# The two meta rows times w_out: fp32 on four column tiles in place of split fp32r

## The chip, the cores and the metric

The kernel runs on one core of one Trainium2 chip. A core has a matrix engine (TensorE, PE in the profile, with its weight loads listed apart as PEld), three engines for elementwise work (VectorE or DVE, ScalarE or ACT, GpSimd or POOL), and queues that issue DMA transfers; here nearly all transfers go through SyncE's queue (SP). The metric is the device time of one execution in microseconds, lower is better; the time of a kernel is the median of its runs.

## The reference

The kernel computes one layer of a hybrid decoder trunk for 1024 tokens of width 1024, with 16 meta tokens put in front. After a first LayerNorm the layer does this:

```python
z = h @ w_in + b_in                      # q, k, v, conv input, gates
y_attn = attention(q, k, v) @ w_attn_proj
y_conv = conv_branch(c_in) @ w_conv_proj
mixed = sigmoid(g_attn) * y_attn + sigmoid(g_conv) * y_conv
h = layer_norm(ALPHA * h + mixed @ w_out, ln1_g, ln1_b)
up = causal_dwconv(h @ ffn_w_up, ffn_dw, ffn_dw_b)      # 3 taps
u, g = split(up)
out = layer_norm(ALPHA * h + (gelu(g) * u) @ ffn_w_down, ln2_g, ln2_b)
```

Only the 1024 token rows are returned. Of the 16 meta rows just the last two are needed behind `mixed`: the causal convolution of the feed-forward part has three taps, so the first token row reaches back to them. These two rows, a 2 x 1024 matrix, have to be multiplied with `w_out` (1024 x 1024) like the 1024 others, and this product is what the change concerns.

## The kernel before

**Numbers in two parts.** Nearly every product is made to fp32 accuracy from fp32r operands. A value `x` is split into `hi`, its fp32r rounding, and `lo = x - hi`; ACT makes `hi` and DVE makes `lo` (`split`, L300 to L303). A product is then three matmuls per block of the contraction: `lo*hi`, `hi*hi`, `hi*lo` (`product`, L340 to L344).

**Order of the work.** The code gives each instruction a rank (`tc.cur_priority`, `rank`), and a planner lays out each engine's instructions by simulated time: whatever is ready and has the lowest rank goes next. Where a fixed order is wanted, `after` ties one instruction behind another. An engine, and a DMA queue, runs its instructions strictly in the order that came out; an instruction that waits holds up those behind it on its engine.

**Stages.** First the projection `z`, then attention and convolution, then the two branch projections with the gates (L1172 on PE, `merge` on DVE and ACT, up to about 506 us), then the row stage (498 to 605 us), then the up product (to 1035 us), then the down product.

**The branch projections** loop over eight blocks `m` of 128 channels and over four groups `g` of token columns. `merge` writes the mixed values, split, to `RHC` and `RHO`. For the first group it also puts the two meta rows aside in the tile `pair`: for each channel block four columns, two of the fp32r part (L1187, ACT) and two of the rest (L1188, DVE).

**The weights** `w_out` are loaded in eight blocks of 128 rows and split by `prep_wo`. Blocks 0 to 3 are loaded into parts of the tile `FA` (`early`, at columns 2064, 3088, 0 and 1024), block 4 into `FA` from column 4112, block 5 into `OB` from column 3072, blocks 6 and 7 into the two buffers `wr` that all weights pass through. The split parts go to `OA`, `RX`, `RW` and `w`. A raw block is free again when it has been split; the next user of the two `wr` buffers is the first block of up weights.

**The row stage** calls `out_rows(i)` for the row blocks in the order 3, -1, 7, 2, 6, 0, 4, 1, 5, where -1 stands for the two meta rows. A row block of 128 is multiplied with `w_out` in two halves of 512 columns, 24 matmuls a half, on a PSUM bank out of a ring of three (`ps_w`, tag `mm`, shared with the projections). DVE adds the residual rows, which were loaded from `h0d` (L1345), and takes the statistics; the block is normalized (L271 to L274 and L1369), written to `h1d`, and turned by PE transposes (L1379) between the halves of a later block. Block 3 is turned between the halves of block 7, block 7 between those of block 2, and the meta rows behind the second half of block 2.

**The meta rows** have their own path in `out_rows` (n = 2, L1355 to L1364). A half is 16 matmuls: per channel block one with all four columns of `pair` as the stationary operand and `hi` of `w_out` as the moving one (L1356), and one with the two fp32r columns and `lo` (L1357). So the bank has four rows: rows 0 and 1 hold `hi*hi + hi*lo`, rows 2 and 3 hold `lo*hi`. ACT copies the four rows to `OB` from column 3072 (L1358). Rows 2 and 3 must be added to rows 0 and 1; since DVE works within a partition, a DMA first moves them to partitions 0 and 1 of `FA` (the load at L1363, added at L1364), as it does for the residual rows of `h0d` (added at L1362).

Of the kernel before, what the change touches and what calls it, by code (L numbers as in the profile page):

```python
# [23 lines left out]
F = mybir.dt.float32  # L24
R = mybir.dt.float32r
AF = mybir.ActivationFunctionType
OP = mybir.AluOpType
AX = mybir.AxisListType

P = 128  # L30
D = 1024
KC = D // P
# [81 lines left out]
def tile_hybrid_layer(  # L114
# [3 lines left out]
    nc = tc.nc  # L118
# [5 lines left out]
    def load(o, i):  # L124
        return nc.sync.dma_start(out=o, in_=i)
# [5 lines left out]
    def f32(ap):  # L131
        return ap.bitcast(F)
# [6 lines left out]
    @contextmanager  # L139
    def rank(p):  # L140

        saved = tc.cur_priority
        tc.cur_priority = p
        yield
        tc.cur_priority = saved


    const = ctx.enter_context(tc.tile_pool(name="const", bufs=1, side="left"))
# [8 lines left out]
    FA = arena.tile([P, 6144], F, name="FA")  # L157
    RHC = arena.tile([P, KC * T], R, name="RHC")
    RHO = arena.tile([P, KC * T], R, name="RHO")
    OB = arena.tile([P, 4 * U], F, name="OB")  # L160
# [8 lines left out]
    h0d = dpool.tile([U, D], F, name="h0d")  # L169
# [11 lines left out]
    start = ExitStack()  # L181
# [114 lines left out]
    def wraw(shape):  # L296
        return wraw_p.tile(shape, F, name="wr", tag="wr")
# [13 lines left out]
    def wsp_flat(dtype=R):  # L311
        t = wsp(dtype)
        return [t[:, o:o + D] for o in W_FLAT]
# [279 lines left out]
    for a, b in ((0, 400), (400, J_LEN)):  # L593
        ps = pat.tile([P, 512], F, name="ps_v", tag="o" if a == 0 else "mm", bufs=1 if a == 0 else 3)
# [204 lines left out]
    ps = pat.tile([P, 512], F, name="ps_vm", tag="t", bufs=2)  # L799
    after(nc.tensor.transpose(ps[:64, :P], vmT, ident), q1[-1])  # L800
    src = ps[:64, :P].rearrange("p (g d) -> p g d", d=HD)
    nc.scalar.copy(vm[:64, :, 0], src)
    nc.vector.tensor_tensor(vm[:64, :, 1], src, f32(vm[:64, :, 0]), OP.subtract)
    for q4 in range(2):
        ps = pat.tile([P, 512], F, name="ps_v4", tag="t", bufs=2)
# [3 lines left out]
        src = ps[:, :].rearrange("p (n g d) -> p n g d", g=2, d=HD)  # L809
        for g in range(NKV):  # L810
            hi, lo = (V[:, q4 * 4:q4 * 4 + 4, g, i] for i in range(2))
# [21 lines left out]
    ps = pat.tile([P, 512], F, name="ps_s2", tag="t", bufs=2)  # L833
    for h in range(NH):
        g, r = divmod(h, 4)
        o = ps[:2, h * 16:(h + 1) * 16]
# [50 lines left out]
    ps = pat.tile([P, 512], F, name="ps_o", tag="o", bufs=1)  # L887
# [16 lines left out]
    for i in range(NB):  # L904
# [5 lines left out]
        for g in range(NKV):  # L910
# [6 lines left out]
            for r in range(4):  # L917
                ps = pat.tile([P, 512], F, name="ps_s", tag="s", bufs=2)
# [11 lines left out]
            hs = slice(g * 4, g * 4 + 4)  # L930
# [9 lines left out]
            for c, kb in bands:  # L940
                ps = pat.tile([P, 512], F, name="ps_t", tag="t", bufs=2)
# [20 lines left out]
    order = [1, "c2"] + list(range(2, 5)) + ["c3"] + list(range(5, 16))  # L962
# [166 lines left out]
        return t[:, 0:8192].rearrange("p (t j x) -> p t j x", t=2, j=2)[:, :, j, cols]  # L1129

    w_out_v = w_out.rearrange("(k p) c -> k p c", p=P)
    wo = {}

    def prep_wo(k, raw=None, behind=None):
        if k < 4:
            hi, lo = (OA[:, OA_WO + k * 2048 + x:OA_WO + k * 2048 + x + 1024] for x in (0, 1024))
        elif k < 6:
            hi, lo = ((RX[:, RX_WO:], RW)[k - 4][:, x:x + 1024] for x in (0, 1024))
        else:
            hi, lo = wsp_flat()  # L1140
        if raw is None:
            raw = wraw([P, D])
            load(raw, w_out_v[k])
        split(raw, hi, lo, behind)
        wo[k] = (hi, lo)

    pair = const.tile([P, KC, 4], R, name="pair")
    g_next = [0]

    GS = [(FA, i * 516) for i in range(4)]  # L1150
# [11 lines left out]
    for m in range(KC):  # L1162
        hi, lo = weights([P, KC, P], lambda raw: load(raw, w_ab[m]))

        def branch(i, g, tag, bufs):
            a, b = PG[g]
            ps = pat.tile([P, 512], F, name="ps_p", tag=tag, bufs=bufs)
            rhs = (oo, conv)[i]
            for k in range(4):
                ah, al = hi[:, 4 * i + k], lo[:, 4 * i + k]  # L1170
                for j, (x, hl) in enumerate(((ah, 0), (ah, 1), (al, 0))):
                    nc.tensor.matmul(ps[:, :b - a], x, rhs(k, hl, a, b), start=k + j == 0, stop=k == 3 and j == 2)  # L1172
            return ps[:, :b - a]

        def merge(g, psa, psb):
            a, b = PG[g]
            n = b - a
            with rank(RK_EVAC):
                t = gslot()[:, :, :n]
                ins = load(t, dram(sgd, m * P * U + a, [[U, P], [KC * P * U, 2], [1, n]]))  # L1180

                ta, tb = t[:, 0], t[:, 1]
                nc.vector.scalar_tensor_tensor(ta, ta, 1.0, psa, OP.add, OP.mult)
                nc.vector.scalar_tensor_tensor(tb, tb, 1.0, psb, OP.add, OP.mult)
                nc.vector.tensor_tensor(ta, ta, tb, OP.add)
                if g == 0:
                    nc.scalar.mul(pair[:, m, 0:2], ta[:, 0:2], 0.5)  # L1187
                    nc.vector.scalar_tensor_tensor(pair[:, m, 2:4], ta[:, 0:2], 0.5, f32(pair[:, m, 0:2]),  # L1188
                                                   OP.mult, OP.subtract)
                v = ta[:, n - 256:].rearrange("p (t x) -> p t x", t=2)  # L1190
                h = mixed2(g, m, 0)
                last_act = nc.scalar.mul(h, v, 0.5)
                nc.vector.scalar_tensor_tensor(mixed2(g, m, 1), v, 0.5, f32(h), OP.mult, OP.subtract)
            return ins, last_act

        if m < KC - 1:
            pa = [branch(0, g, "mm", 3) for g in range(2)]
            for g in range(4):
                if g > 1:
                    pa.append(branch(0, g, "mm", 3))  # L1200
                last_gate, last_act = merge(g, pa[g], branch(1, g, "t", 2))
        else:
            pa = [branch(0, g, "mm", 3) if g < 3 else branch(0, g, "s", 2) for g in range(4)]
            for g in range(4):
                last_gate, last_act = merge(g, pa[g], branch(1, g, "t", 2))
        if m in (2, 3):
            raw = (FA[:, 4112:5136], OB[:, 3072:4096])[m - 2]
            load(raw, w_out_v[m + 2])
            prep_wo(m + 2, raw, last_act)
        if m < 4:  # L1210
            early.append(FA[:, E_AT[m]:E_AT[m] + 1024])
            after(load(early[m], w_out_v[m]), last_gate)
# [109 lines left out]
    def out_rows(i, between=(), work=()):  # L1322


        n, u = (P, 2 + i * P) if i >= 0 else (2, 0)
        if n == P:
            o = r_next[0] % 2 * 1024
            r_next[0] += 1
            whole = RT[:, o:o + 1024]
            load(whole, h0d[u:u + n, :])  # L1330
        else:
            whole = OB[:, 3072:4096]
        r = whole[:n]
        order = WO_ORDER if i != 5 else (0, 1, 2, 3, 6, 7, 4, 5)
        turned = None
        st = small.tile([P, 2, 6], F, name="st")
        pin = line if i in (0, 4, 1, 5) else lambda ins: ins
        for half in range(2):
            hs = slice(half * 512, half * 512 + 512)
            ps = pat.tile([P, 512], F, name="ps_w", tag="mm", bufs=3)  # L1340
            if n == P:
                last = product(ps, [(mixed(i, k, 0), mixed(i, k, 1), wo[k][0][:, hs], wo[k][1][:, hs])
                                    for k in order], turned)
                with rank(RK_TURN):
                    pin(nc.vector.tensor_tensor(r[:, hs], ps, r[:, hs], OP.add))  # L1345
                    pin(nc.vector.bn_stats(st[:, half], r[:, hs]))
                turned = None
                if len(between) > half:
                    turned = turn(*between[half], behind=[last])
                if half == 0:  # L1350
                    for f, *x in work:
                        f(*x)
                continue

            for j, k in enumerate(order):  # L1355
                nc.tensor.matmul(ps[:4], pair[:, k], wo[k][0][:, hs], start=j == 0, stop=False)  # L1356
                last = nc.tensor.matmul(ps[:2], pair[:, k, 0:2], wo[k][1][:, hs], start=False, stop=j == KC - 1)  # L1357
            nc.scalar.copy(whole[:4, hs], ps[:4])  # L1358
        if n < P:
            q = FA[:4, 0:1024]  # L1360
            load(q[0:2], h0d[0:2, :])
            nc.vector.tensor_tensor(r, r, q[0:2], OP.add)  # L1362
            load(q[0:2], whole[2:4])  # L1363
            nc.vector.tensor_tensor(r, r, q[0:2], OP.add)  # L1364
        with rank(RK_TURN):
            (mu, rs), = ln_stats([(r, n)], half_stats=st if n == P else None)
            for a in (512, 0) if i == 5 else (None,):
                x = r if a is None else r[:, a:a + 512]
                ins = pin(nc.vector.tensor_scalar(x, x, mu, rs, OP.subtract, OP.mult))  # L1369
        if n == P:  # L1370
            load(h1d[u - 2:u - 2 + P, :], r)
        return whole, n, ins
# [198 lines left out]
    for c in range(FC):  # L1571
        V4, X, Z, Y = (pup.tile([P, 1024], F, name=n, tag=n) for n in ("pw", "px", "pz", "py"))
        passes = ((1,), (0,)) if c == 0 else ((0, 1),)
        for subs in passes:
            last = subs == passes[-1]
# [317 lines left out]
```

## Time and profile before

| | us |
|---|---|
| median of 3 runs (device time) | 1254.46 |
| the runs | 1253.59, 1254.46, 1257.59 |
| the profiled execution, from its first to its last instruction (its span) | 1253.2 |
| PE busy in the span | 1239.1 (99%) |
| DVE busy | 1078.1 (86%) |
| ACT busy | 627.4 (50%) |
| first meta matmul to the first matmul of row block 7 | 510.27 to 519.08 |

The profile is of one execution. Of that execution only the span is known; its device time is not listed apart. The rows below are of four kinds. A row of the groups gives line, engine, operation, output and inputs, shape and count, then busy time, mean duration in ns, and idle time ahead. A row of the waits gives engine, tile and line, what it waited for, then total, times and longest. A row of the timeline gives start, duration, engine, line, operation, shape and count, and in brackets the idle time before it with what ended it. A row of one line's view gives minimum, median and maximum duration in ns and first and last start. `SPq` is the issue of a DMA on SyncE's queue, all recorded at the helper's line L125. Matmuls are pipelined: a record covers a matmul from its start to its modelled end, and the next can start well before that end.

### The profile page before, as it was taken

The page shows a single profiled execution, that of the slowest core. Times are in us where ns is not written, and L with a number is a line of the kernel's source. Part 1 is how long each engine was busy: PE and PEld are TensorE (multiplying, and loading weights), DVE is VectorE, ACT ScalarE, POOL GpSimd, SP SyncE. Part 2 cuts the span into 40 slices and gives each one's busy share as a digit, 9 for nine tenths or more (in the row PEclk, how much of TensorE's full clock was granted, in tenths as well). Part 3 has the DMA queues.
Part 4 walks back from the last instruction along what each step waited for, and adds up shares of the span by engine and source line. Part 5 has one row for each costly group of instructions (what it writes and reads, how often), then busy time and mean ns, then how long its engine had stood idle before and what let it go on. Part 6 is the DMA issues. An engine that isn't in the chain of part 4 may idle for free.

```text
span 1253.2 us, 23194 instructions
## 1 busy us (share of the span) xinstructions
PE 1239.1 (99%) x9176; PEld 1173.8 (94%) x9176; DVE 1078.1 (86%) x1862; ACT 627.4 (50%) x1284; POOL 7.4 (1%) x8
## 2 busy tenths in 40 slices
PE   8999999999999999999999999999999999999997
PEld 7999999999999999788899999999999998888886
DVE  8989999999978677448899999998999977896697
ACT  8533255655474233344676556565565654545330
POOL 0000000001000000000000000000000000000000
PEclk9999999999999999999999999999999999999999
DMA  7383633432256564222145555453454567998712
GB/s 261 117 292 102 191 93 98 109 95 81 73 157 173 170 164 119 85 94 75 68 160 191 194 197 201 161 211 137 163 206 175 196 227 251 395 342 330 276 60 84
DMA packets 98687, 212.20 MB, mean 169 GB/s; under 512 B 11395, under 2 KB 38595, under 8 KB 98322
## 3 DMA queue, kind: packets, MB, share of 16 engines
q1 hardware_dynamic: 84414, 199.57, 46.9%
q10 hardware_dynamic: 14164, 11.15, 2.8%
q8 instruction: 72, 1.18, 0.4%
q14 instruction: 37, 0.30, 0.1%
HBM read 150.29 MB, written 62.70 MB: 170 GB/s over the span
## 4 chain that ended last, share of the span: by engine, by line
PE 96%; DVE 2%; ACT 1%; DMA 1%; issue 0%; SPq 0%; DVEq 0%; ACTq 0%
PE px L1594 15%; PE py L1594 10%; PE ps_x L1739 9%; PE ps_z L340 8%; PE ps_z L343 8%; PE ps_z L344 8%; PE ps_z L1739 7%; PE ps_p L1172 7%; PE pz L1594 5%; PE pw L1594 5%; PE ps_w L344 2%; PE ps_w L343 2%; PE ps_w L340 2%; PE ps_z L575 2%; PE ps_t L943 1%; PE ps_s L919 1%
## 5 line engine op out<-in xcount | busy, mean ns | idle before, releaser
L340 PE MATMUL ps_z<-RHO,w 128*128 128x256 f32 (+2 forms) x864 | 243.2, 281 | 0.0
L343 PE MATMUL ps_z<-RHO,w 128*128 128x256 f32 (+2 forms) x864 | 242.3, 280 | 0.0
L344 PE MATMUL ps_z<-RHC,w 128*128 128x256 f32 (+2 forms) x864 | 242.2, 280 | 0.0
L343 PEld LDWEIGHTS ps_z<-RHO,w 128*128 128x128 f32 x864 | 162.5, 188 | 0.5
L344 PEld LDWEIGHTS ps_z<-RHC,w 128*128 128x128 f32 x864 | 162.7, 188 | 0.2
L340 PEld LDWEIGHTS ps_z<-RHO,w 128*128 128x128 f32 x864 | 162.5, 188 | 0.1
L749 DVE SCALAR_TENSOR_TENSOR FA<-cin,cdw,FA 128x1026 f32<-128x1026 f32 x120 | 154.3, 1295 | 0.7
L300 ACT CAST w<-wr 128x1024 fp32r<-128x1024 f32 x37 | 38.8, 1048 | 64.0 <-PE ps_z L344 48.0
L1412 DVE TENSOR_TENSOR RHO<-wr,RHO 128x512 fp32r<-128x512 f32 x94 | 64.0, 684 | 3.6 <-ACT RHO L1411 3.5
L1411 ACT CAST RHO<-wr 128x512 fp32r<-128x512 f32 x94 | 56.9, 619 | 15.6 <-DVE wr L1429 7.9
L1429 DVE TENSOR_TENSOR wr<-wr 128x512 f32<-128x512 f32 x88 | 60.1, 683 | 0.1
L758 ACT ACTIVATE FA<-ps_z,colr 128x258 f32<-128x258 f32 (+1 forms) x64 | 30.1, 472 | 59.0 <-PE ps_z L344 50.7
L303 DVE TENSOR_TENSOR w<-wr,w 128x1024 fp32r<-128x1024 f32 x37 | 45.1, 1218 | 7.6 <-ACT w L300 7.4
L1606 ACT COPY FA<-px 128x516 f32<-128x516 f32 (+2 forms) x23 | 13.1, 571 | 71.2 <-PE px L1594 71.2
L1172 PE MATMUL ps_p<-OC,w 128*128 128x256 f32 (+1 forms) x384 | 48.1, 278 | 0.0
L1172 PE MATMUL ps_p<-OA,w 128*128 128x256 f32 (+1 forms) x384 | 47.8, 278 | 0.0
L1172 PEld LDWEIGHTS ps_p<-OC,w 128*128 128x128 f32 x384 | 46.2, 188 | 0.1
L1172 PEld LDWEIGHTS ps_p<-OA,w 128*128 128x128 f32 x384 | 45.9, 188 | 0.0
L1412 DVE TENSOR_TENSOR w<-wr,w 128x512 fp32r<-128x512 f32 x60 | 40.7, 684 | 4.7 <-ACT w L1411 4.7
L1594 PE MATMUL px<-OA,RHO 128*128 128x260 f32 x324 | 43.0, 282 | 0.0
L1594 PE MATMUL px<-OC,RHO 128*128 128x256 f32 x324 | 41.2, 276 | 0.8 <-DVE OB L1345 0.8
L1594 PE MATMUL px<-RHC,RHO 128*128 128x256 f32 (+1 forms) x312 | 40.6, 279 | 0.1
(457 smaller groups left out, 3109.3 us busy)
## 6 DMA issues: line engine op xcount, KB each, us to landing
wr<-in_w_up_dram SPq DMA_DIRECT2D x44, 512.0 KB, 3.6
wr<-in_w_z_dram SPq DMA_DIRECT2D x29, 512.0 KB, 4.2
OB<-in_w_down_dram SPq DMA_DIRECT2D x24, 512.0 KB, 5.2
fd<-FA SPq DMA_DIRECT2D x44, 256.0 KB, 2.0
FA<-sd SPq DMA_DIRECT2D x15, 512.0 KB, 8.9
qt<-qd SPq DMA_DIRECT2D x28, 256.0 KB, 4.1
OB<-td SPq DMA_DIRECT2D x14, 512.0 KB, 8.7
sgd<-FA ACTq DMA_DIRECT2D x48, 128.0 KB, 2.4
```

Source lines behind the costliest of these rows:

```text
L300: ins = nc.scalar.copy(hi, raw)
L303: return nc.vector.tensor_tensor(lo, raw, f32(hi), OP.subtract)
L340: ins = nc.tensor.matmul(ps, al, bh, start=i == 0, stop=False)
L343: nc.tensor.matmul(ps, ah, bh, start=False, stop=False)
L344: last = nc.tensor.matmul(ps, ah, bl, start=False, stop=i == n - 1)
L749: nc.vector.scalar_tensor_tensor(acc[c], cin[:, j:j + U], wc, acc[c], OP.mult, OP.add)
L1172: nc.tensor.matmul(ps[:, :b - a], x, rhs(k, hl, a, b), start=k + j == 0, stop=k == 3 and j == 2)
L1411: nc.scalar.copy(hi, src)
L1412: ins = nc.vector.tensor_tensor(lo, src, f32(hi), OP.subtract)
L1429: ins = nc.vector.tensor_tensor(*x)
L1594: ins = nc.tensor.matmul(o, (ah, ah, al)[j][:, k * P:(k + 1) * P], bmat(sub, q, j, k), start=first and i == 0, stop=i == 11, skip_group_ch ...
L1739: nc.tensor.matmul(banks[i], l[:, ts], r[:, ws], start=first and a and x + k == 0, stop=z and x == len(ops) - 1 and k == 2, skip_group_che ...
```

## The change

The meta rows are kept in plain fp32, and multiplied with the raw, unsplit blocks of `w_out`, also in plain fp32. The tile `pair` holds two columns per channel block, one block behind the other, and 32 columns of zeros at the end; the stationary operand of block `k` is the 32 columns from column `2k`, of which the first two are those of block `k`. Block `k` writes the 32 PSUM partitions from `32 * (k % 4)`, so blocks 0 and 4 add up in partitions 0 to 31, blocks 1 and 5 in partitions 32 to 63, and so on. The rows 0 and 1, 32 and 33, 64 and 65, and 96 and 97 hold the four partial sums; the other rows hold values that nothing reads. A half is 8 matmuls in place of 16. ACT copies all 128 partitions. The residual rows and the three other partial sums are brought to partitions 0 and 1 by four DMAs, in two slots of `FA` that alternate, and added by four DVE instructions.

The raw blocks must now live until the meta matmuls have read them. Because block 5 lies in `OB` from column 3072, the rows' own place moves to `OB` from column 2048. The splits of `w_out` stay, as the row blocks of 128 still use them.

```diff
-    wo = {}
+    wo, wo_raw = {}, {}
...
         split(raw, hi, lo, behind)
-        wo[k] = (hi, lo)
-
-    pair = const.tile([P, KC, 4], R, name="pair")
+        wo[k], wo_raw[k] = (hi, lo), raw
+
+    pair = const.tile([P, 2 * KC + 32], F, name="pair")
+    nc.vector.memset(pair[:, 2 * KC:], 0.0)
...
                 if g == 0:
-                    nc.scalar.mul(pair[:, m, 0:2], ta[:, 0:2], 0.5)
-                    nc.vector.scalar_tensor_tensor(pair[:, m, 2:4], ta[:, 0:2], 0.5, f32(pair[:, m, 0:2]),
-                                                   OP.mult, OP.subtract)
+                    nc.scalar.mul(pair[:, 2 * m:2 * m + 2], ta[:, 0:2], 0.5)
...
         else:
-            whole = OB[:, 3072:4096]
+            whole = OB[:, 2048:3072]
...
-            for j, k in enumerate(order):
-                nc.tensor.matmul(ps[:4], pair[:, k], wo[k][0][:, hs], start=j == 0, stop=False)
-                last = nc.tensor.matmul(ps[:2], pair[:, k, 0:2], wo[k][1][:, hs], start=False, stop=j == KC - 1)
-            nc.scalar.copy(whole[:4, hs], ps[:4])
+            for k in range(KC):
+                o = k % 4 * 32
+                nc.tensor.matmul(ps[o:o + 32], pair[:, 2 * k:2 * k + 32], wo_raw[k][:, hs], start=k < 4, stop=k >= 4)
+            nc.scalar.copy(whole[:, hs], ps)
         if n < P:
-            q = FA[:4, 0:1024]
-            load(q[0:2], h0d[0:2, :])
-            nc.vector.tensor_tensor(r, r, q[0:2], OP.add)
-            load(q[0:2], whole[2:4])
-            nc.vector.tensor_tensor(r, r, q[0:2], OP.add)
+            for j, src in enumerate((h0d[0:2, :], whole[32:34], whole[64:66], whole[96:98])):
+                q = FA[:2, j % 2 * 1024:j % 2 * 1024 + 1024]
+                load(q, src)
+                nc.vector.tensor_tensor(r, r, q, OP.add)
```

## The prediction

> **What bounds the kernel now.** I read the page from its first part to the chain of waits, then the waits of PE, then the stretch around the two changed matmul lines instruction by instruction on each engine.
>
> ```profile
> span 1253.2 us, 23194 instructions
> PE 1239.1 (99%) x9176; PEld 1173.8 (94%) x9176; DVE 1078.1 (86%) x1862; ACT 627.4 (50%) x1284; POOL 7.4 (1%) x8
> PE 96%; DVE 2%; ACT 1%; DMA 1%; issue 0%; SPq 0%; DVEq 0%; ACTq 0%
> ```
>
> PE is busy for 99% of the span and makes up 96% of the chain that ended last. So PE time taken out of the row stage is worth its full length, unless a wait appears in its place; work of DVE, ACT or a queue costs nothing until PE waits for it. The waits of PE:
>
> ```profile
> PE pw L1594 <- ACT FA L1392: 1.2, 1, 1.2
> PE px L1594 <- DVE OB L1345: 0.8, 1, 0.8
> ```
>
> Those are its two longest after the opening of the kernel, and both lie past 600 us, where the up product starts. In the stage that the change touches PE waits for nothing. The stage itself:
>
> ```profile
> 510.27 0.40 PE L1356 MATMUL ps_w<-RX,pair 128*4 128x512 f32 x1
> 510.97 0.40 PE L1357 MATMUL ps_w<-RW,pair 128*2 128x512 f32 x1
> 511.20 0.39 PE L340 MATMUL ps_w<-w,RHC 128*128 128x512 f32 x1
> 512.12 0.40 PE L1356 MATMUL ps_w<-OA,pair 128*4 128x512 f32 x1
> 512.36 0.40 PE L1357 MATMUL ps_w<-OA,pair 128*2 128x512 f32 x1
> 512.59 0.63 PE L344 MATMUL ps_w<-w,RHC 128*128 128x512 f32 x2
> 513.05 0.39 PE L1356 MATMUL ps_w<-OA,pair 128*4 128x512 f32 x1
> 518.84 0.40 PE L1357 MATMUL ps_w<-w,pair 128*2 128x512 f32 x1
> 519.08 0.40 PE L340 MATMUL ps_w<-RX,RHC 128*128 128x512 f32 x1
> ```
>
> Columns: start, duration, engine and line, tiles, shape. The 32 matmuls of the two meta rows run in three pieces: four from 510.27, two from 512.12, twenty-six from 513.05 to 519.08, where the product of row block 7 begins. A record lasts 0.40 us, but starts follow each other at 6.03 / 26 = 0.232 us: records overlap, and the distance of the starts is the price.
>
> **The change, part by part.**
>
> *Removed from PE:* 32 matmuls at 0.232 = 7.42 us, all on the path.
>
> *Added to PE:* 16 matmuls of 512 columns whose operands are plain fp32 (no fp32r), each writing 32 partitions. The nearest rows are the plain fp32 matmuls of the first projections:
>
> ```profile
> L572 PE MATMUL ps_z<-FA,wr x32: 392/393/497, 12.6 to 21.2; 128*128 128x272 f32 x32
> 15.89 5.67 PE L572 MATMUL ps_z<-FA,wr 128*128 128x272 f32 x24
> 21.40 1.47 PE L518 MATMUL ps_h<-coll,xn 128*128 128x128 f32 x12
> ```
>
> L572 is called 16 times (8 blocks of the contraction, tiles 0 and 1), and the trace holds 32 records: a plain fp32 matmul is two matmul records. Twenty-four of them take 21.40 - 15.89 = 5.51 us, 0.230 us for 272 columns, so 0.230 x 512 / 272 = 0.432 us a record and 0.864 us a matmul. Nothing in this trace writes column tiles, so how far they run side by side is the unknown. Bounds:
> - all four side by side: 32 x 0.432 / 4 = 3.46 us (a gain of 3.96);
> - none: 32 x 0.432 = 13.82 us (a loss of 6.40).
>
> I take a value between. The two records of one matmul need the same 32 columns, so the second can only stream when the first is through; and in the rows above PE starts matmuls one after the other in program order. The code puts neighbouring tiles next to each other call by call, not record by record. In order, the second record of tile 0 waits for its first, and the first record of tile 1 stands behind it; then these two go together, and so on: two at a time, one matmul per 0.432 us, 17 x 0.432 = 7.35 us for the block in one piece. That is the old 7.42 to within 0.1.
>
> On the order the Trainium skill says the same in "TensorE: Matmul & The Clock Gate", Part 3, "The mechanism": weight loads may be pulled ahead, but matmuls start and end strictly in program order. On the parallelism it speaks for the change: the same part states a 2.38 times speed for three column tiles, and "TensorEngine Tiling (Array Packing)", Key Properties, says that tiles "operate independently". By the second rule alone the block would be the 3.46 us of the first bound; no row of this trace has column tiles, so neither is confirmed here, and the choice above goes by the rows.
>
> *Pieces and switches.* The planner put the meta matmuls into holes where row block 3 waited for the last split weights; I take three pieces again. With two at a time, each further piece loses one 0.432 of overlap: +0.86. A change from the full array to column tiles and back may let the array empty: at most 0.40 - 0.232 = 0.16 us by the rows above, six times 1.0, at least 0; I take half, 0.5, as no end is nearer. (The Trainium skill, "TensorEngine Tiling (Array Packing)", Key Properties, says that switching the tiling mode drains TensorE; the trace shows no such switch.) Block: 7.35 + 0.86 + 0.5 = 8.7; change on PE +1.3 us, between -3.96 and +6.40 + 1.0 = +7.4.
>
> *ACT's two copies* now move 128 partitions instead of 4:
>
> ```profile
> 515.57 0.57 ACT L1358 COPY OB<-ps_w 4x512 f32<-4x512 f32 x1 [8.11 <-PE ps_w L1357]
> 519.27 0.57 ACT L1358 COPY OB<-ps_w 4x512 f32<-4x512 f32 x1 [1.52 <-PE ps_w L1357]
> L1411 ACT CAST RHO<-wr 128x512 fp32r<-128x512 f32 x94 | 56.9, 619 | 15.6 <-DVE wr L1429 7.9
> ```
>
> A 128-partition copy of 512 elements takes 0.62, so +0.05 each at most, covered by ACT's idle 8.11 and 1.52.
>
> *The sum of the four parts* stands on DVE and SP, off PE:
>
> ```profile
> 497.03 0.25 SPq L125 DMA_DIRECT2D FA<-h0d  x1
> 519.88 1.21 DVE L1362 TENSOR_TENSOR OB<-OB,FA 2x1024 f32<-2x1024 f32 x1 [0.70 <-ACT OB L1358]
> 521.12 0.70 SPq L125 DMA_DIRECT2D FA<-OB  x1
> 523.19 1.21 DVE L1364 TENSOR_TENSOR OB<-OB,FA 2x1024 f32<-2x1024 f32 x1 [2.09 <-DMA FA<-OB]
> 529.91 0.28 ACT L271 ACTIVATE sd<-mv,eps 2x1 f32<-2x1 f32 x1
> 531.70 0.79 DVE L1369 TENSOR_SCALAR OB<-OB,mv,sd 2x1024 f32<-2x1024 f32 x1
> 542.68 0.60 PE L1379 MATMUL ps_h<-coll,OB 128*128 128x128 f32 x4
> ```
>
> Before: one residual load (early, at 497.03), one fold: 2.07 us from issue to its reader, two adds of 1.21. After: four loads and four adds. The residual load now waits for the matmuls, since its place in FA holds raw weights until then; the four loads alternate between two slots, so the third waits for the first add. Counted as if nothing overlapped, two more load-and-add steps are 2 x (2.07 + 1.21) = 6.6 us, and the late residual load one more 2.07. The normalized meta rows were ready at 531.70 + 0.79 = 532.5, PE transposes them at 542.68: cover 10.2 us against 8.7. So nothing on PE; without that cover it would be the 8.7 itself. In truth the loads of different slots overlap, and the rows waited for ACT until 529.91 anyway.
>
> While DVE waits for those loads, the adds of row block 7 stand behind:
>
> ```profile
> 525.64 0.66 DVE L1345 TENSOR_TENSOR OB<-ps_w,OB 128x512 f32<-128x512 f32 x1
> 531.09 0.69 DVE L1345 TENSOR_TENSOR OB<-ps_w,OB 128x512 f32<-128x512 f32 x1 [0.36 <-PE ps_w L344]
> 534.28 0.81 DVE L1369 TENSOR_SCALAR OB<-OB,mv,sd 128x1024 f32<-128x1024 f32 x1
> 536.33 1.03 PE L1379 MATMUL ps_h<-coll,OB 128*128 128x128 f32 x8
> ```
>
> The first of them has from 525.64 to the second at 531.09, 5.5 us; the block is normalized at 535.09 and turned at 536.33, 1.24 us of cover. I cost it at nothing.
>
> *Raw weights kept longer.* The raw tiles of blocks 6 and 7 were free for the first up weights once split; now they wait for the last meta matmul:
>
> ```profile
> 492.11 0.34 SPq L125 DMA_DIRECT2D wr<-in_w_up_dram  x1
> 506.70 0.34 SPq L125 DMA_DIRECT2D OB<-h0d  x1
> 508.30 0.33 SPq L125 DMA_DIRECT2D wr<-in_w_up_dram  x1
> 564.25 0.66 ACT L1411 CAST RHO<-wr 128x512 fp32r<-128x512 f32 x1
> ```
>
> The two loads go from 492.11 and 508.30 to about 519; the first reader is at 564.25, 45 us later. Nothing, if they also move in SP's queue (a rival below).
>
> *DVE and ACT before the stage.* Eight L1188 instructions go, one memset comes:
>
> ```profile
> 500.55 0.16 DVE L1188 SCALAR_TENSOR_TENSOR pair<-OB,pair 128x2 fp32r<-128x2 f32 x1
> 1.48 0.17 DVE L239 MEMSET ones<- 128x128 f32 x1
> ```
>
> 8 x 0.16 = 1.3 us off DVE, 0.17 at most on: no wait of PE hangs on either. Nothing.
>
> Sum: +1.3 us on the span, 1254.5. The median of the three runs, 1254.46, stands 1.26 above the span, and a measurement of this kernel can tell about 0.3%, 3.8 us, from no change. Predicted median: 1254.46 + 1.3 = **1255.8**.
>
> **The rivals.**
>
> 1. *All four tiles run side by side.* For it: the code alternates the tiles, and a queue per tile would let tile 1 begin while tile 0 holds its second record. Against: starts in program order. In one piece the block is 3.46, the time 1250.5; in three pieces (say 2, 1 and 13 calls) 0.86 + 0.86 + 3.46 = 5.2 and 0.5 for the switches, 1252.7.
>
> 2. *No overlap (slower).* The full-array rows run one after the other at 0.432 a record, and column tiles may too. It gives 13.82 + 0.5 - 7.42 = +6.9: 1261.4. It decides as soon as the block takes more than 7.42 + 3.8 = 11.2 us, an overlap below 13.82 / 11.2 = 1.23.
>
> 3. *The held tile blocks SP's queue.* If the planner leaves the first up load (492.11) ahead of row block 3's residual load (506.70), that load goes out at about 519 and not 506.70. Its readers:
>
> ```profile
> 513.59 1.29 DVE L1345 TENSOR_TENSOR OB<-ps_w,OB 128x512 f32<-128x512 f32 x2 [4.99 <-DMA OB<-h0d]
> 518.37 0.81 DVE L1369 TENSOR_SCALAR OB<-OB,mv,sd 128x1024 f32<-128x1024 f32 x1
> 524.56 1.03 PE L1379 MATMUL ps_h<-coll,OB 128*128 128x128 f32 x8
> ```
>
> Row block 3 would be normalized 12.4 us later than 519.18, at 531.6, and PE would wait from 524.56 on: +7.0, with the +1.3 a time of 1262.8. Against it: the loads of before stand in the order in which their places came free. A smaller form is DVE's: a load wait of 2.07 and an add of 1.21 falling right ahead of row block 7's second half cost 3.28 - 1.24 = +2.0, 1257.8.
>
> **How the numbers follow.** Two at a time 0.40; rival 1 0.24; rival 2 0.22; rival 3 0.14. Under 1250.7 (faster by 0.3%) ends rival 1 only in one piece: 0.17. Within: the rest of rival 1 (0.07) and the forecast (0.38). Over 1258.2: rivals 2 and 3 (0.36) and 0.02 of the forecast, where pieces and waits add up. Range: from 1250.4, the full overlap, to 1262.0, no overlap with all six switches at their bound (+7.4); the forecast's own range is 1254.4 (one piece, no drain) to 1257.8 (with the DVE wait).
>
> **What would show it.** In the profile of the changed kernel the line of the new matmul has 32 records. Right: from the first to the last start some 8 us in all pieces, starts in pairs 0.43 us apart. Starts four at a time, or a stretch near 3.5 us, is rival 1; a start every 0.43 us is rival 2. The up loads should stand behind row block 7's residual load on SP; the waits of PE should name no L1345 or L1369 before 545 us. The transposes of the meta rows should come with no idle time before them. A wait there, or a planner that spreads the 16 calls over many pieces, makes the prediction wrong.

## The result: slower by 10 us, and the profile after

The changed kernel takes 1264.78 us (median; its times go from 1264.39 to 1264.89) against 1254.79 of the kernel before (1254.46 above, with one run fewer): a ratio of 1.008, with a 95% interval of 1.0068 to 1.0092. The span went from 1253.2 to 1263.1 us. The prediction said 1255.8, with a range up to 1262.0.

The page of the changed kernel, with the same three lines as before:

```profile
span 1263.1 us, 23203 instructions
PE 1250.5 (99%) x9176; PEld 1181.3 (94%) x9176; DVE 1078.8 (85%) x1857; ACT 626.6 (50%) x1284; POOL 7.4 (1%) x8
PE 96%; DVE 2%; ACT 1%; DMA 0%; issue 0%; DVEq 0%; SPq 0%; ACTq 0%
```

PE has as many matmul records as before (9176), is busy for the same 99% of the span, and makes up the same 96% of the chain. Yet its busy time grew by 11.4 us. So the time did not go into waiting. PE's two longest waits behind the opening are those of before, to a tenth of a microsecond:

```profile
PE pw L1592 <- ACT FA L1390: 1.2, 1, 1.2
PE px L1592 <- DVE OB L1344: 0.8, 1, 0.8
```

Next the place of the change, the timeline of PE in the changed kernel:

```profile
511.39 1.06 PE L1356 MATMUL ps_w<-FA,pair 128*32 128x512 f32 x6
512.38 0.50 PE L340 MATMUL ps_w<-w,RHC 128*128 128x512 f32 x1
...
513.50 1.05 PE L1356 MATMUL ps_w<-FA,pair 128*32 128x512 f32 x4
514.48 0.73 PE L344 MATMUL ps_w<-w,RHC 128*128 128x512 f32 x2
515.15 0.62 PE L1356 MATMUL ps_w<-OB,pair 128*32 128x512 f32 x1
515.15 0.62 PE L1356 MATMUL ps_w<-wr,pair 128*32 128x512 f32 x2
515.60 0.59 PE L1356 MATMUL ps_w<-OB,pair 128*32 128x512 f32 x1
515.61 0.60 PE L1356 MATMUL ps_w<-wr,pair 128*32 128x512 f32 x2
515.77 1.48 PE L1356 MATMUL ps_w<-FA,pair 128*32 128x512 f32 x9
...
517.85 0.50 PE L340 MATMUL ps_w<-RX,RHC 128*128 128x512 f32 x1
```

The 32 records stand in three pieces, and each piece is short: 512.38 - 511.39 = 0.99 us for 6 records, 0.98 for 4, and 517.85 - 515.15 = 2.70 for 22. That is 4.67 us where the old block had 0.93 + 0.47 + 6.03 = 7.43. From the first meta matmul to the first of row block 7 it is 517.85 - 511.39 = 6.46 us, against 8.81 before: **the block became 2.3 us shorter**. So some 12 us were lost elsewhere, and the stage that was changed does not show them.

They show when the same piece of work is laid side by side in both chains of waits (columns: start, length, engine, tile and line, count of matmuls). Before:

```profile
412.23 85.81 PE ps_p L1172 x744
...
645.85 2.79 PE px L1594 x24
...
1035.45 29.95 PE ps_z L1739 x132
```

After (the lines moved by two or one):

```profile
411.30 87.64 PE ps_p L1173 x744
...
645.74 2.85 PE px L1592 x24
...
1041.87 30.48 PE ps_z L1737 x132
```

The 744 matmuls of the branch projections, which nobody touched, take 1.83 us more; 24 matmuls of the up product 0.06 more; 132 of the down product 0.53 more. The loss is 1.8 to 2.2% in each of these rows. The rows of the tile `OC`, which these stages read, tell more (minimum, median and maximum of a matmul in ns). Before:

```profile
L1594 PE MATMUL py<-OC,RHO x156: 276/276/276, 638.8 to 1029.6; 128*128 128x256 f32 x156
L1739 PE MATMUL ps_x<-OC,RHO x144: 389/389/389, 1081.8 to 1184.9; 128*128 128x512 f32 x144
```

After:

```profile
L1592 PE MATMUL py<-OC,RHO x156: 278/281/286, 638.5 to 1036.0; 128*128 128x256 f32 x156
L1737 PE MATMUL ps_x<-OC,RHO x144: 393/394/399, 1088.9 to 1194.0; 128*128 128x512 f32 x144
```

Before, all 156 and all 144 are alike to the nanosecond; after, each single one is longer. But not every group became slower. Groups of before, by shape (busy us and mean ns behind the bar):

```profile
L340 PE MATMUL ps_z<-RHO,w 128*128 128x256 f32 x648 | 181.3, 280 | 0.0
L1594 PE MATMUL px<-OC,RHO 128*128 128x256 f32 x324 | 41.2, 276 | 0.8 <-DVE OB L1345 0.8
```

and of after:

```profile
L340 PE MATMUL ps_z<-RHO,w 128*128 128x256 f32 x648 | 181.5, 280 | 0.0
L1592 PE MATMUL px<-OC,RHO 128*128 128x256 f32 x324 | 43.0, 282 | 0.8 <-DVE OB L1344 0.8
```

`RHO` with `w` kept its 280 ns; `OC` with `RHO` went from 276 to 282.

What these two groups differ in can be read from where the tiles lie in on-chip memory. Old `pair` took 8 x 4 x 4 = 128 bytes of each partition, new `pair` takes (16 + 32) x 4 = 192. It is allocated ahead of the large tiles of the left side, so `FA`, `RHC`, `RHO`, `w`, `OA` and all others behind it moved by 64 bytes (`RHO` from 87136 to 87200, `w` from 9952 to 10016, in the built programs). The tiles of the right side, `OC` (195456), `RX` and `RW`, stayed. `RHO` and `w` moved together; between `OC` and `RHO` the distance changed by 64.

That gave the first theory: **the pace of a matmul depends on the distance between its two operands in memory, and the 64 bytes of `pair` cost the 12 us.** The rivals: the column tiles leave something behind that slows later matmuls, or the new order of instructions does.

### The profile page after: what moved, and what is told of

It reads as the page before. It is cut to its first block, busy times and chain, and to the rows that moved or that the text cites. A ratio compares the mean times of both kernels' runs of the same rounds, so it can differ in the third digit from the quotient of the medians.

```text
span 1263.1 us, 23203 instructions
## 1 busy us (share of the span) xinstructions
PE 1250.5 (99%) x9176; PEld 1181.3 (94%) x9176; DVE 1078.8 (85%) x1857; ACT 626.6 (50%) x1284; POOL 7.4 (1%) x8
## 4 chain that ended last, share of the span: by engine, by line
PE 96%; DVE 2%; ACT 1%; DMA 0%; issue 0%; DVEq 0%; SPq 0%; ACTq 0%
PE px L1592 15%; PE py L1592 10%; PE ps_x L1737 9%; PE ps_z L340 8%; PE ps_z L343 8%; PE ps_z L344 8%; PE ps_z L1737 7%; PE ps_p L1173 7%; PE pz L1592 5%; PE pw L1592 5%; PE ps_w L340 2%; PE ps_w L344 2%; PE ps_w L343 2%; PE ps_z L575 2%; PE ps_t L943 1%; PE ps_z L572 1%
## 5 line engine op out<-in xcount | busy, mean ns | idle before, releaser
L1409 ACT CAST RHO<-wr 128x512 fp32r<-128x512 f32 x94 | 56.8, 618 | 13.3 <-DVE wr L1427 6.4
L1604 ACT COPY FA<-px 128x516 f32<-128x516 f32 (+2 forms) x23 | 13.1, 571 | 76.1 <-PE px L1592 76.1
L1592 PEld LDWEIGHTS px<-OC,RHO 128*128 128x128 f32 x324 | 40.2, 188 | 1.2 <-DVE OB L1344 1.2
```

The source lines that it names most:

```text
L1409: nc.scalar.copy(hi, src)
L1592: ins = nc.tensor.matmul(o, (ah, ah, al)[j][:, k * P:(k + 1) * P], bmat(sub, q, j, k), start=first and i == 0, stop=i == 11, skip_group_ch ...
```

## Experiments on the cause

**e1_same_place.** The change in full, but 16 unused columns ahead of `pair` are taken out, so that everything behind `pair` lies where it lay before.

```diff
-    coll = const.tile([P, n_kept - n_right + 24], F, name="coll")[:, :n_kept - n_right]
+    coll = const.tile([P, n_kept - n_right + 8], F, name="coll")[:, :n_kept - n_right]
```

> The changed kernel with 16 unused floats taken out of the tile coll, which lies ahead of pair, so that every tile behind pair has the address that it has in the kernel before. The instructions and their order are those of the changed kernel. Theory A (the 64 bytes by which pair grew move all tiles of the left side, and PE reads a moving and a stationary operand more slowly or faster by how they lie to each other): the 256-column matmuls of the up product go from 119 back to 116 ns apart, and only the gain of the meta block is left, 2.3 us: 1252.5. Rival B (the new work itself, its DMAs, adds and longer held raw tiles, costs the 10 us in a way that the waits don't name): 1264.8 as measured for the change.

Measured: 1253.13 us, ratio 0.9985 (0.9975 to 0.9994), span 1251.6. The chain of e1 has the old lengths:

```profile
413.13 85.81 PE ps_p L1173 x744
...
644.57 2.79 PE px L1592 x24
...
1034.17 29.95 PE ps_z L1737 x132
```

In the built programs its instructions stand in the same order as those of the changed kernel on every engine, and its column tiles are the same. So neither the column tiles nor the order slow the other stages; the place of the tiles does, and it was worth 1263.1 - 1251.6 = 11.5 us.

**e2_before_moved.** The other way round: the kernel before, with `pair` made 64 bytes longer and nothing else.

```diff
-    pair = const.tile([P, KC, 4], R, name="pair")
+    pair = const.tile([P, KC, 6], R, name="pair")[:, :, :4]
```

> The kernel before with nothing but 16 unused floats a partition behind pair, which moves the tiles of the left side by 64 bytes as the change does. Theory A: some 1450 matmuls of 256 columns lose 5 ns each and some 590 of 512 columns 6 ns each, 7.3 + 3.5 = 10.8 us: 1265.6. Rival B: no change, 1254.8.

Measured: 1266.88 us, ratio 1.0102 (1.0087 to 1.0117), span 1265.2: 12.0 us for 64 unused bytes. Its chain:

```profile
411.09 87.64 PE ps_p L1172 x744
...
647.67 2.85 PE px L1594 x24
...
1044.09 30.48 PE ps_z L1739 x132
```

These are the three lengths of the changed kernel. The spans are of single executions, and their openings differ by up to 2 us (the first rows of the chains start between 411.09 and 413.13). So the accounts are better kept from that row to the end of the span: 841.0 us before, 851.8 after, 838.5 in e1, 854.1 in e2. The place then costs 13.1 us (e2 against before) or 13.3 (after against e1); 13.1 less 2.3 for the block is 10.8, and the changed kernel took 10.8 more than the kernel before.

**e3_after_128 and e4_both_sides** ask whether it is the distance or the address of one side. e3 moves the left side on by another 64 bytes, 128 in all. e4 leaves it at 64 and moves the right side by 64 the other way; so the distance changes by 128 in both, with different addresses.

```diff
 e3
-    pair = const.tile([P, 2 * KC + 32], F, name="pair")
+    pair = const.tile([P, 2 * KC + 48], F, name="pair")[:, :2 * KC + 32]
 e4
-    half_ = constr.tile([P, 1], F, name="half")
+    half_ = constr.tile([P, 24], F, name="half")[:, 0:1]
```

> The changed kernel with 16 more unused floats behind pair, so that the left side lies 128 bytes from its place in the kernel before and not 64. Theory A with a period of 128 bytes: as with the old addresses, 1252.5. Theory A with a longer period (256 bytes or more): slow as the change or otherwise, 1258 to 1266. Rival B: 1264.8.

> The changed kernel with the tiles of the right side (OC, RX, RW and others) moved down by 64 bytes too, so that left and right lie to each other as in the kernel before, modulo 128, while every address has moved by 64. If the pace hangs on how the two operands lie to each other: 1252.5. If it hangs on where an operand itself lies (its own address modulo 128): the moved OC and the moved weights are both off their old places, at least as slow as the change, 1264.8 or more. Rival B: 1264.8.

Measured: e3 1264.92 (1.0082, 1.0067 to 1.0097), e4 1262.95 (1.0068, 1.0051 to 1.0084). The old pace does not come back at 128 bytes. By their times alone the two don't decide between distance and address. To compare them I sorted the spacings from one fp32r matmul to the next by the distance from the moving operand of the first to the stationary operand of the second, in bytes modulo 256 (starts from the traces, addresses from the built programs; spacings that hold a wait, over 150 and 300 ns, left out):

```
            256 columns, ns (count)              512 columns, ns (count)                 sum, us (256; 512)
before      64: 114.3 (4845)                      0: 227.0 (1287)                         560.0; 315.3
e1          64: 114.3 (4845)                      0: 226.9 (1282)                         560.0; 306.6
after       64: 114.7 (3415)  128: 119.0 (1459)   0: 227.9 (690)   64: 233.2 (521)        568.8; 310.3
e2          64: 114.7 (3415)  128: 119.0 (1458)   0: 228.0 (696)   64: 233.2 (526)        568.5; 319.6
e3          64: 114.8 (3443)  192: 117.8 (1434)   0: 228.0 (697)  128: 232.8 (590)        567.2; 310.9
e4          64: 114.9 (3443)  192: 117.8 (1434)   0: 228.0 (697)  128: 232.8 (590)        567.2; 310.9
```

(Groups of under 140 are not shown but are in the sums. The sums of before and e2 at 512 columns hold the 32 old meta matmuls too, 7.4 us.) In e3 and e4 the tiles lie at different addresses and at the same distances, and each spacing agrees within 0.1 ns; from the branch projections to the end both take 850 us, alike within 0.1. So it is the distance. From e1 to after, 8.8 us come from the matmuls of 256 columns and 3.7 from those of 512: 12.5 of the 13.3. Most of the rest, 0.7, is in matmuls of 260 columns. That the whole span grew by 11.5 only is due to the opening, where e1 has a wait of 2.1 us (`ps_h`, L518) that the profile of after has not.

**e9_distance and e10_four_places** measure this cost by itself. They leave out the whole layer and were run once each: two tiles `M` and `W` of one repeated input, and rows of ten matmuls at each pair of offsets.

```diff
 e10 (e9: a in (0, 8), 48 values of d)
+    for n in (256, 512):
+        for a in (0, 2, 4, 6):
+            for d in range(16):
+                for i in range(10):
+                    mm(ps[:, :n], W[:, 8 * d:8 * d + P], M[:, 8 * a:8 * a + n], start=i == 0, stop=i == 9)
```

> Not the layer, but a measure of the disputed cost by itself: ten fp32r matmuls each for 256 and for 512 columns, for two places of the moving operand 256 bytes apart, and for 48 places of the stationary operand in steps of 32 bytes. Theory (the pace hangs on the distance of the two operands): the distance between starts changes by 3 to 6 ns with the place of the stationary operand, the pattern moves by 256 bytes with the moving operand, it is best at a distance of 64 bytes for 256 columns and of 0 for 512, and it repeats after 512 bytes. Rival (own address of one operand): the pattern doesn't move with the moving operand. If the pace is the same everywhere, the cause lies elsewhere in the kernel, as in the writes of ACT and DVE to the moved tiles.

> As e9_distance, not the layer: sixteen places of the stationary operand in steps of 32 bytes, for four places of the moving operand 0, 64, 128 and 192 bytes into its tile. e9_distance has shown a pattern with a period of 256 bytes, and could not tell a distance from an address, since its two places of the moving operand lie one period apart. If the distance sets the pace, the fast place for 256 columns (113.4 ns) goes with the moving operand: 64, 128, 192 and 256 bytes into the tile of the stationary operand; for 512 columns (229 ns and below) 0, 64, 128, 192. If the stationary operand's own address sets it, the fast place stays at 64 and at 0. If the two together set it in another way, the table shows that.

Measured: e9 showed a period of 256 bytes in the stationary operand's place, not the 512 that I had expected; its two places of the moving one were 256 apart and gave the same pattern, so it could not tell a distance from an address. e10 could. Rows of ten in e10's timeline at 256 columns, the stationary operand at 0, 64 and 128 bytes into its tile, the moving one at 0:

```profile
17.05 1.35 PE L31 MATMUL ps<-M,W 128*128 128x256 f32 x10
...
19.42 1.30 PE L31 MATMUL ps<-M,W 128*128 128x256 f32 x10
...
21.76 1.34 PE L31 MATMUL ps<-M,W 128*128 128x256 f32 x10
```

and the same with the moving one at 64:

```profile
35.92 1.34 PE L31 MATMUL ps<-M,W 128*128 128x256 f32 x10
...
38.27 1.35 PE L31 MATMUL ps<-M,W 128*128 128x256 f32 x10
...
40.64 1.30 PE L31 MATMUL ps<-M,W 128*128 128x256 f32 x10
```

The short row moved along by 64, from the second to the third. From start to start it is 113.3 ns in it and 117.8 to 119.1 in the others. At 128 and 192 the short row is again the one in which the stationary operand lies 64 further on (modulo 256). At 512 columns the rows are less clear: distance 0 takes 226.7 to 230.2 ns in the mean, 192 takes 228.9 to 230.0 (in one case 233.3), and 64 and 128 cost 231.8 to 233.9. So 0 and 192 can hardly be told apart here, as ten matmuls are few: in most rows at 0 the first spacings run from 224 to 236 ns and only the last two are at 226 to 227, the mean that the layer has at 0 (its 133 spacings at 192 in after have 230.2). Offsets of an odd multiple of 32 bytes cost 117.2 to 120.4 and 232.8 to 233.6. The granted clock is 1.00 in all these rows, and no other engine works in them; so neither the clock nor writes of ACT and DVE to the moved tiles are needed for the effect.

What follows: the distance sets the pace, by 3 to 7 ns a matmul, with a period of 256 bytes. Open is which pair of operands meets: counting by each matmul's own two operands instead sorts the layer's spacings equally well, as neighbours mostly use the same tiles. What in the hardware makes it was not shown either. A shift by a full 256 bytes was not tried in the layer; the left and right side have only 128 bytes between them.

## Experiments on the block itself

All of these lie at the old addresses, so they are compared with e1.

**e7_one_tile.** All 16 calls on the first column tile, one sum in place of four.

```diff
-                o = k % 4 * 32
-                nc.tensor.matmul(ps[o:o + 32], pair[:, 2 * k:2 * k + 32], wo_raw[k][:, hs], start=k < 4, stop=k >= 4)
-            nc.scalar.copy(whole[:, hs], ps)
+                nc.tensor.matmul(ps[0:32], pair[:, 2 * k:2 * k + 32], wo_raw[k][:, hs], start=k == 0, stop=k == KC - 1)
+            nc.scalar.copy(whole[:32, hs], ps[:32])
...
-            for j, src in enumerate((h0d[0:2, :], whole[32:34], whole[64:66], whole[96:98])):
+            for j, src in enumerate((h0d[0:2, :],)):
```

> The changed kernel at the old addresses, with all 16 calls on column tile 0, each half summed in one place. There is only one partial sum, so three of the four loads and adds go and 32 partitions are copied. Theory (the four tiles run side by side, and that is the whole gain of the new product): the calls follow each other at 2 x 0.432, 13.8 us in place of 4.68, 9.1 us more than e1_same_place: 1262.3. If the tiles never overlapped in the changed kernel, or if its loads and adds cost time on the path: no more than 1253.1.

Measured: 1262.64 us, 1.0064 (1.005 to 1.0078), span 1261.4. The timeline of e7:

```profile
518.27 4.46 PE L1355 MATMUL ps_w<-FA,pair 128*32 128x512 f32 x10
...
522.56 1.02 PE L1355 MATMUL ps_w<-OB,pair 128*32 128x512 f32 x2
```

Ten records from 518.27 to 522.56 are 0.429 us each: the estimate of 0.432 was right, and on one tile the records follow at that full price. The pieces are 1.83 + 0.98 + 11.28 = 14.1 us, 9.4 more than e1's; the span is 9.8 longer. That these agree so well is partly luck: from the branch projections on e7 takes 11.7 us more, with 1.3 us of waits in the down product (`ps_z`, L1736) that e1 has not, and a shorter opening made up for it. So the four tiles do bring a gain, of two thirds of the block.

**e6_one_piece.** e1 with the first meta matmul tied behind the last matmul of row block 3, so that there is one piece.

```diff
+    row_mm = []
...
                 last = product(ps, ...)
+                row_mm.append(last)
...
-                nc.tensor.matmul(ps[o:o + 32], ...)
+                ins = nc.tensor.matmul(ps[o:o + 32], ...)
+                if k == 0 and half == 0:
+                    after(ins, row_mm[-1])
```

> The changed kernel at the old addresses (as in e1_same_place), with the first meta matmul ordered behind the last matmul of row block 3, so that the 16 calls stand in one piece and not in three. Theory: a piece costs what its fullest tile holds, and each way in or out of column tiles some 0.1 us. The three pieces of e1_same_place take 0.99 + 0.98 + 2.71 = 4.68 us, one piece 32 x 0.432 / 4 = 3.46 and 0.2, with four switches fewer by 0.4: 1.4 us less than e1_same_place, 1251.7. Rival: the holes in row block 3 are real waits for the last split weights, PE stands still in them, and nothing is gained: 1253.1.

Measured: 1251.65 us, 0.9974 (0.9965 to 0.9983), span 1250.9. The timeline of e6:

```profile
512.40 1.47 PE L1358 MATMUL ps_w<-FA,pair 128*32 128x512 f32 x9
...
515.97 0.50 PE L340 MATMUL ps_w<-RX,RHC 128*128 128x512 f32 x1
...
534.38 1.06 PE L1381 MATMUL ps_h<-coll,OB 128*128 128x128 f32 x8 [0.90 <-issue]
```

515.97 - 512.40 = 3.57 us for 32 records, 0.112 each: 0.429 / 0.112 = 3.8 times the pace of one tile. That is the first bound of the prediction (3.46), and rival 1 in one piece. Row block 7 begins 1.8 us earlier than in e1 (515.97 against 517.74): 0.2 lie at the opening, 1.1 are the block's, and the 0.4 left fit two pieces fewer, each with a way in and a way out at 0.1. The span gained only 0.7, because a wait appeared: row block 7 is turned 0.90 us late. The profile names no releaser for it (`issue`), but DVE had to normalize the meta rows before it:

```profile
532.17 0.80 DVE L1371 TENSOR_SCALAR OB<-OB,mv,sd 2x1024 f32<-2x1024 f32 x1
...
533.47 0.81 DVE L1371 TENSOR_SCALAR OB<-OB,mv,sd 128x1024 f32<-128x1024 f32 x1
```

DVE is done with block 7 at 533.47 + 0.81 = 534.28, no earlier than in the changed kernel (534.26), while PE is there at 534.38 - 0.90 = 533.48 and not at 535.36. That is the small form of rival 3, with the cover used up by PE's earlier arrival; e11 below tests it.

**e8_tile_by_tile.** e1 with the calls in another order, so that both calls of a tile stand one behind the other.

```diff
-            for k in range(KC):
+            for k in (0, 4, 1, 5, 2, 6, 3, 7):
```

> The changed kernel at the old addresses, with the blocks taken in the order 0, 4, 1, 5, 2, 6, 3, 7, so that four records in a row are for the same tile. If PE starts matmul records strictly in program order, only the last of a tile and the first of the next overlap: 32 - 7 = 25 records of 0.432, 10.8 us in place of 4.68: 1259.2. If each tile takes up its records on its own, however the program mixes them: as e1_same_place, 1253.1. In between, if PE looks ahead by a few records.

Measured: 1255.32 us, 1.0004 (0.9995 to 1.0013), span 1253.8. The timeline of e8:

```profile
510.14 1.90 PE L1356 MATMUL ps_w<-FA,pair 128*32 128x512 f32 x4
511.97 0.50 PE L340 MATMUL ps_w<-w,RHC 128*128 128x512 f32 x1
...
515.61 1.25 PE L1356 MATMUL ps_w<-FA,pair 128*32 128x512 f32 x6
516.50 0.60 PE L1356 MATMUL ps_w<-wr,pair 128*32 128x512 f32 x2
...
519.20 0.50 PE L340 MATMUL ps_w<-RX,RHC 128*128 128x512 f32 x1
```

Here the first two pieces hold records of one tile each and run serially, 1.83 us for four. The third has 24 records, in the built program always four of one tile in a row, and takes 519.20 - 515.61 = 3.59 us = 8 x 0.43 and 0.15: the length of the tile with most records. Started in program order, it could not have been that short. Even a whole call is overtaken: block 6 stands ahead of block 3 in the program, but block 3 is one of the `FA` records at 515.61 (the first two are blocks 2 and 3), and block 6, from `wr`, begins at 516.50. So a tile takes up its records on its own, and what counts is how many records each tile has in a piece. How far ahead PE looks was not measured. The pieces add up to 7.25 us, 2.6 more than e1's; the span is 2.2 longer. The time lies between the two forecasts, 1253.1 and 1259.2: the first of them did not reckon with pieces that hold a single tile at a time.

**e11_fold_later.** e6, with the partial sums added and the meta rows normalized only behind row block 7 in the code.

```diff
+        def finish():
             if n < P:
                 for j, src in enumerate((h0d[0:2, :], whole[32:34], whole[64:66], whole[96:98])):
...
-        return whole, n, ins
+            return whole, n, ins
+        return finish() if n == P else finish
...
-            two = (i, *out_rows(i))
+            fold = out_rows(i)
...
         if i == 7:
-            ahead.append(two)
+            ahead.append((-1, *fold()))
```

> As e6_one_piece, with the fold of the four parts and the norm of the meta rows written behind row block 7 in the code, so that on DVE the norm of row block 7 goes ahead of that of the meta rows. In e6_one_piece PE waited 0.90 us at the transposes of row block 7, a wait that the kernel before does not have. Theory (DVE held row block 7's norm back by the meta rows' own steps, 0.80 for their normalization and some 0.5 for small ones): the wait goes, 0.9 us less than e6_one_piece's 1251.65, 1250.8, and no new wait at the transposes of the meta rows, which come 6 us later. Rival (the wait comes from PE reaching row block 7's transposes too soon for the work of DVE that hangs on row block 7 alone): the wait stays at 0.9.

Measured: 1251.19 us, 0.9974 (0.9964 to 0.9985), span 1249.4. The wait of 0.90 is gone:

```profile
532.17 1.03 PE L1384 MATMUL ps_h<-coll,OB 128*128 128x128 f32 x8
```

So the wait did come from the order of DVE's work. The span is 1.5 us below e6's, but that is not this wait alone: 1.1 lie ahead of the branch projections, 1.1 between there and the up product (the wait of 0.9 is among them), and 0.7 are lost again behind it; what lost them was not followed up. The two medians, 1251.19 and 1251.65, can't be told apart by their intervals. Both versions beat the kernel before, by some 3 us.

## Why the prediction was wrong, point by point

**The step that failed: "DVE and ACT before the stage ... one memset comes ... Nothing."** It counted the instructions that write `pair`, but gave the tile itself no line in the sum. The diff shows it growing from 32 to 48 columns; that this moves every tile behind it was not thought of, and neither the range nor any rival held a cost outside the row stage. It cost 12.0 us of span (e2), 13.1 from the branch projections on. No row of the profile before would have priced it, since nearly all its matmuls have one distance per shape. But a scale could have been had from rows that the prediction quotes: with 9176 records, one nanosecond more for each is 9 us.

**"Two at a time, one matmul per 0.432 us": failed as well, in the other direction.** The price of a record held (0.429 in e7). The overlap was four, not two. I had read from the full-array rows that matmuls start in program order and carried this over to column tiles. In the changed kernel the rows at 515.15 show three records, of blocks 5, 6 and 7, starting together, and the second record of block 5 follows only at 515.60: the first records of two later calls start ahead of the second of an earlier one. Whole calls still start in the program's order there; in the third piece of e8 a whole call is overtaken too. The Trainium skill's rule in "TensorE: Matmul & The Clock Gate", Part 3, "The mechanism", that matmuls start strictly in program order, thus does not hold across column tiles here; "TensorEngine Tiling (Array Packing)", Key Properties, that tiles operate independently, does: 3.57 us against 14.1 on one tile. Nor does the sentence above that an engine runs its instructions strictly in order hold for PE across column tiles.

**Pieces and switches.** Three pieces were right. They cost 4.67 - 3.57 = 1.1 us (0.86 was said), as a piece that doesn't fill all tiles evenly ends with its fullest. The switch was said at 0.5 for all six and at most 0.16 each. The records of after show 0.32 from the last full matmul to the first of the block (511.07 to 511.39) and 0.33 from the first full one behind it to the next (512.38 to 512.71), where 0.23 is usual: 0.1 each, 0.6 in all. But column tiles as such don't cost it. "Nothing in this trace writes column tiles" was wrong, and so was "the trace shows no such switch": in the built program of the kernel before, the old meta matmuls already have a tile of 32 columns, the first, and PE goes into it and out at the usual 0.23 (510.05 to 510.27, 518.84 to 519.08). In e7, on that same first tile, the way in from the full matmul is 0.32 again (509.02 to 509.34). So the 0.1 comes with the new plain fp32 calls; whether their type or their 32 columns make it was not tried apart.

So the block was said at 8.7 and is, with its switches, some 5.3: rival 1 in three pieces (1252.7), which e1 gives with 1253.13. In one piece the rival said 1250.5; e6 gave 1251.65 and e11 1251.19.

**The hidden steps were right.** ACT's copies, the four loads and adds, and the raw weights held longer cost PE nothing: no wait that was not there before. The loads of up weights moved behind both residual loads on SP's queue, as the last part of the prediction expected. The queue in the changed kernel:

```profile
507.71 2.26 SPq L125 DMA_DIRECT2D OB<-h0d  x2
517.10 0.25 SPq L125 DMA_DIRECT2D FA<-h0d  x1
517.96 1.42 SPq L125 DMA_DIRECT2D wr<-in_w_up_dram  x2
519.43 1.47 SPq L125 DMA_DIRECT2D FA<-OB  x2
```

**Rival 2** is ruled out by the block's 4.67 us. Its price was near: a single tile costs 14.1 us in its three pieces (e7), 13.82 + 0.5 was said. **Rival 3** did not come in the changed kernel, since the up loads at 517.96 are behind the residual loads at 507.71; its small form, DVE's work for the meta rows ahead of row block 7's, came in e6 with 0.90 us in place of 2.0.

That the time came out on the slower side is thus no support for either slower rival: the price was paid in stages that the prediction didn't look at.

## What to carry to other kernels

When a diff changes the size of a tile, look at what lies behind it in memory: where a kernel is bound by TensorE, keep the distances between operands as they were (or choose them) before judging the change, and repeat the old kernel with the new tile size, as in e2. If busy time grows with the same number of matmuls and the same waits, compare the same groups in untouched stages first. For small products like this one, give every column tile an equal share of each uninterrupted piece: here a piece lasted as long as its fullest tile.

## What the runs showed of the hardware

- The pace of fp32r matmuls depends on the distance of their operands in memory, modulo 256 bytes: with 256 columns 113 to 115 ns at a distance of 64 bytes and 117 to 120 else (e10 and the layer); with 512 columns 227 to 230 at 0 and 232 to 234 at 64 and 128.
- Four column tiles of 32 run plain fp32 side by side: 32 records of 512 columns in 3.57 us, where one tile takes 0.429 us a record; each tile takes up its own records, ahead of earlier ones that wait for another tile.
- Going from full-array fp32r matmuls to plain fp32 ones on column tiles, and back, costs about 0.1 us each time (0.32 and 0.33 where 0.23 is usual). Going to fp32r matmuls on the first column tile and back costs nothing that shows (0.23, before).
